# PE transposes for short segments, a doubling step in pairs, and a factor moved, in a planned fp32 decoder kernel

## The chip, the cores and the metric

One core of one Trainium2 chip runs the kernel. The metric is the device time of one execution in microseconds (us), the median of several executions. Engines are named as the profile names them: PE (TensorE matmul) with PEld (its weight loads), DVE (VectorE), ACT (ScalarE), POOL (GpSimd) and SP (the queue that issues most transfers).

## The reference

One inference step of a one-layer hybrid decoder, all in fp32. A prompt of 16 meta tokens and 512 tokens and a sample group of 8 sequences of 4 tokens go through the layer together, so the kernel works on 560 columns (544 after the meta tokens are dropped).

```python
h = rms_norm(x, g_mix)
proj = h @ w_in        # GLU a | GLU b | q | k | v | z | beta | decay | gate_conv | gate_delta
c = silu(layer_norm(depthwise_conv31(glu_a * sigmoid(glu_b)) + b_dw)) @ w_cout
q, k, v = split(silu(depthwise_conv4(qkv)))      # 8 heads x 128, q and k L2-normalised
# gated delta rule in chunks of tokens; per head, with state S (128 x 128):
M = beta * (k @ k.T) * decay;  A = tril(M, -1) + I
value, kcum = solve(A, [v * beta, k * beta * exp(G)])
u = value - kcum @ S
o = (q * exp(G)) @ S + ((q @ k.T) * decay) @ u
S = S * exp(G_last) + (k * exp(G_last - G)).T @ u
x = x + (sigmoid(gate_c) * c + sigmoid(gate_d) * (rms_norm(o) * silu(z)) @ w_dout) @ w_o
x = x + relu(rms_norm(x) @ w_up) ** 2 @ w_down
```

The prompt's rows start from S = 0; the 8 sample sequences start from states that are read in, 8 x 8 x 128 x 128 numbers, and are written back updated.

## The kernel before, in words

**Large products.** Every weight matrix is cut into chunks of 128 output channels. A chunk's fp32 weights are split into a rounded high part (`wh`) and the remainder (`wl`), the activations likewise, and three products are added: in `gemm` (L613) 88 chunks of 8 x 3 x 2 matmuls of 272 to 280 columns, each one pass; in `up_gemm` (L2083) and `dn_gemm` (L2234) the channel mixer in the same manner. `weights_prep` makes `wl` of a chunk in one of two ways: for chunks `A0` to `A1` - 1 ACT writes -`wh` and POOL issues a transfer that adds the weights to it (L579, L581); for the others DVE subtracts (L585). Results go to two PSUM tiles `pg` in turn, which an evacuation empties.

**The delta rule** uses fp32 matmuls on small tiles; one such matmul stands in the trace as two records. The prompt is solved in segments of 128 tokens (4 per head, the index j), the 48 leftover columns (32 sample, 16 meta) as a fifth. `solve` inverts 32x32 blocks on DVE, `doubling` joins them to 64 and then 128: in its second step 32 matmuls of 64x64 read rows 0 to 63 and write partitions 64 to 127 (L1108), their results are copied out by ACT and DVE in turn, and 32 more read rows 64 to 127 and write partitions 0 to 63 (L1119). `head_prep` turns k and v of a head into token rows: the full segments by PE transposes (L1452, L1461), the short ones (`v4`, `k4`) by matmuls against the identity (L1411, L1413). It also makes `at` = (k.q) * s * D from the products of L1469 (L1473, four DVE operations) and `kd`, k scaled by s * ed. `chain` walks the four segments of a head: k S and q S (L1503, L1505), R = v - ... (DVE, L1509), T R (L1518), u copied out by ACT (L1520), kd u (L1522) and at u (L1525), the new S and the output o (DVE L1529, L1532; for j = 0 DVE L1535 and ACT L1537). The four 128-column quarters of one PSUM bank `bx` hold these results; L1503 writes the quarter that L1525 wrote in the step before, so it also waits until o was read from it. Then come the sample sequences: their states `S0` (read by a transfer, L1599) enter matmuls (L1546), and `decode_state` scales them (ACT L1626), adds the update (PE L1621, DVE L1629) and stores them (L1634); the next head's states are read into the same place after that store has landed. `head_post` normalises the head's output and transposes it back (L1660; the short segment by a 48-column matmul, L1669).

**The order of the work.** All of this is written as generators (streams) that a planner, `Weaver`, interleaves when the program is built. Each `op(engine, cost, deps)` has a cost in us; the planner keeps a clock per engine and always takes the stream whose next operation can start first, ties going to the smaller priority. The large products have priority 5 on PE, so small matmuls go between them as soon as the plan says that they can start. What comes out is one fixed sequence per engine; on the chip each engine follows its sequence and waits on semaphores where the plan was wrong. The conv over 31 taps (`conv`, L1217, 240 operations) fills DVE in the same manner.

## Time and profile before

| | us |
|---|---|
| median of 3 runs | 1069.06 (1068.16 to 1070.02) |
| the profiled execution | 1068.65 |
| its span, first to last instruction | 1066.9 |
| PE busy in the span | 1048.2 |
| DVE / ACT busy | 769.4 / 622.9 |

The span is shorter than the time of the same execution by 1.75 us, which lie around it. PE is busy almost always, and the granted clock is 0.995 over the span. Busy time of PE hides how its matmuls overlap (each is busy for some 290 ns and the next starts some 130 ns later), so the distance between the starts of successive rows is what a piece of work takes of PE.

### The profile page before, as it was taken

What the parts mean: (1) busy time and instruction counts of PE and PEld (TensorE: products, weight loads), DVE (VectorE), ACT (ScalarE), POOL (GpSimd) and SP (SyncE); (2) the same over time, 40 slices, a digit from 0 to 9 for tenths busy, and PEclk for the clock granted to TensorE, in tenths of its full rate; (3) what the DMA queues carried; (4) which work ended last, traced back from release to release, by engine and by line L of the source; (5) the groups of instructions that cost most, each with busy time, mean ns of one, the idle gap of its engine ahead of it and who ended that gap; (6) DMA issues with size and microseconds to landing.
All of it is one profiled execution on the core that took longest, in us unless ns stands there. A gap on an engine that the chain in (4) does not pass through costs nothing.

```text
span 1066.9 us, 21819 instructions
## 1 busy us (share of the span) xinstructions
PE 1048.2 (98%) x8835; PEld 1026.1 (96%) x8835; DVE 769.4 (72%) x1360; ACT 622.9 (58%) x1285; POOL 148.1 (14%) x173
## 2 busy tenths in 40 slices
PE   8999999999999999999999999999999999999997
PEld 6988999999999999899999999999999999999996
DVE  5888879788889887788953355778657547746754
ACT  5677334668787878776358424578327426723741
POOL 2067311102211221122111000000000000000000
PEclk9999999999999999999999999999999999999998
DMA  6232687467576566667877522654365365346222
GB/s 213 82 89 70 124 178 164 87 148 161 139 172 164 143 137 156 164 166 182 187 163 158 179 84 91 163 153 117 109 177 129 100 153 149 94 124 164 80 61 84
DMA packets 57872, 145.55 MB, mean 136 GB/s; under 512 B 14612, under 2 KB 20140, under 8 KB 57772
## 3 DMA queue, kind: packets, MB, share of 16 engines
q1 hardware_dynamic: 46828, 104.32, 30.4%
q0 software_dynamic: 10944, 39.85, 23.2%
q8 instruction: 69, 1.13, 0.4%
q14 instruction: 31, 0.25, 0.1%
HBM read 135.14 MB, written 9.01 MB: 135 GB/s over the span
## 4 chain that ended last, share of the span: by engine, by line
PE 87%; DVE 5%; ACT 3%; DMA 3%; issue 2%; SPq 0%; POOL 0%; POOLq 0%; DVEq 0%; ACTq 0%
PE pg L613 42%; PE pg L2234 17%; PE bk L2083 15%; DVE acc L815 1%; DMA pre<-in_sq_dram 1%; DVE V L1217 1%; PE pg L2083 1%; PE bk L1419 1%; PE bk L1518 1%; PE bk L978 1%; DVE of L815 1%; PE bk L1522 1%; PE bk L1503 1%; DMA M<-in_xT_dram 1%; PE bk L1525 1%
## 5 line engine op out<-in xcount | busy, mean ns | idle before, releaser
L613 PE MATMUL pg<-R,wh 128*128 128x280 f32 (+2 forms) x1920 | 279.3, 295 | 1.0 <-ACT pre L803 1.0
L613 PEld LDWEIGHTS pg<-R,wh 128*128 128x128 f32 x1920 | 253.7, 189 | 3.9 <-issue 1.5
L1217 DVE SCALAR_TENSOR_TENSOR V<-V,vec,V 128x512 f32<-128x512 f32 x240 | 180.5, 781 | 2.2
L568 ACT ACTIVATE wh<-wraw 128x1024 fp32r<-128x1024 f32 (+1 forms) x89 | 93.4, 1049 | 94.3 <-PE pg L613 79.3
L613 PE MATMUL pg<-R,wl 128*128 128x280 f32 (+2 forms) x960 | 144.0, 294 | 0.3 <-issue 0.3
L613 PEld LDWEIGHTS pg<-R,wl 128*128 128x128 f32 x960 | 128.5, 189 | 1.8 <-issue 1.4
L581 POOL DMA_DIRECT2D wl<-in_w_dram x60 | 52.6, 876 | 343.8 <-ACT wl L579 252.5
L2014 ACT ACTIVATE whm<-RT 128x512 fp32r<-128x512 f32 x73 | 45.2, 625 | 53.0 <-PE pg L2234 34.8
L579 ACT ACTIVATE wl<-wh 128x1024 fp32r<-128x1024 f32 x60 | 63.5, 1058 | 14.8 <-PE pg L613 12.9
L1969 POOL DMA_DIRECT2D RT<-in_wu_dram x16 | 13.8, 865 | 381.6 <-DMA RT<-in_wu_dram 185.6
L2017 DVE TENSOR_TENSOR wlm<-RT,whm 128x512 fp32r<-128x512 f32 x73 | 49.8, 687 | 16.9 <-issue 8.4
L2234 PE MATMUL pg<-RD,whm 128*128 128x272 f32 (+2 forms) x272 | 57.7, 288 | 0.0
L2234 PE MATMUL pg<-K,whm 128*128 128x272 f32 (+2 forms) x272 | 57.6, 288 | 0.0
L2083 PE MATMUL bk<-R,whm 128*128 128x272 f32 x318 | 54.5, 288 | 0.0
L613 PE MATMUL pg<-K,wh 128*128 128x272 f32 x256 | 53.0, 289 | 0.2 <-DVE K L1766 0.2
L613 PE MATMUL pg<-RD,wh 128*128 128x272 f32 x256 | 53.2, 289 | 0.0
L2234 PE MATMUL pg<-RD,M 128*128 128x272 f32 x264 | 46.2, 288 | 0.0
L2014 ACT ACTIVATE whm<-wrawm 128x512 fp32r<-128x512 f32 x43 | 26.7, 623 | 32.6 <-PE pg L2234 29.7
L2083 PEld LDWEIGHTS bk<-R,whm 128*128 128x128 f32 x318 | 45.6, 189 | 0.0
L585 DVE TENSOR_TENSOR wl<-wraw,wh 128x1024 fp32r<-128x1024 f32 x28 | 35.1, 1253 | 13.5 <-ACT wh L568 9.5
L2234 PE MATMUL pg<-RD,wlm 128*128 128x272 f32 (+2 forms) x272 | 43.5, 289 | 0.0
L2234 PEld LDWEIGHTS pg<-K,whm 128*128 128x128 f32 x272 | 43.5, 188 | 0.0
(524 smaller groups left out, 2442.5 us busy)
## 6 DMA issues: line engine op xcount, KB each, us to landing
wraw<-in_w_dram SPq DMA_DIRECT2D x87, 512.0 KB, 3.8
wl<-in_w_dram POOLq DMA_DIRECT2D x60, 512.0 KB, 5.6
RT<-in_wu_dram SPq DMA_DIRECT2D x24, 512.0 KB, 5.2
RT<-in_wu_dram POOLq DMA_DIRECT2D x16, 512.0 KB, 7.3
wrawm<-in_wn_dram SPq DMA_DIRECT2D x16, 512.0 KB, 3.6
RT<-in_wn_dram SPq DMA_DIRECT2D x16, 512.0 KB, 3.5
M<-in_sd_dram SPq DMA_DIRECT2D x16, 256.0 KB, 3.4
out_osd_dram<-M SPq DMA_DIRECT2D x16, 256.0 KB, 3.8
```

Source lines behind the costliest of these rows:

```text
L568: nc.scalar.activation(wh[:, c[0]:c[1]], w[:, c[0]:c[1]], AF.Copy)
L579: nc.scalar.activation(wl, wh.bitcast(F32), AF.Copy, scale=-1.0)
L581: nc.gpsimd.dma_start(wl, i["w"][n].bitcast(F32R), accum_op=ALU.add)
L585: nc.vector.tensor_tensor(wl, w, wh.bitcast(F32), op=ALU.subtract)
L613: nc.tensor.matmul(pt[:, hf, 0:N], w[idx][:, k, :], x[:, off + hf * N:off + hf * N + N], start=k == 0 and not part and x is hi, stop=k == ...
L815: nc.vector.scalar_tensor_tensor(acc[:, 0:584], pr[:, q:q + 584], vcol(w + q), acc[:, 0:584], op0=ALU.mult, op1=ALU.add)
L1217: nc.vector.scalar_tensor_tensor(cc[:, 0:512], G[r][:, 16 + q:528 + q], vcol(w + q), cc[:, 0:512], op0=ALU.mult, op1=ALU.add)
L1969: nc.gpsimd.dma_start(rb, i["wu"][g][:, 1024:2048], accum_op=ALU.add)
L2014: nc.scalar.activation(hi, raw, AF.Copy)
L2017: nc.vector.tensor_tensor(lo, raw, hi.bitcast(F32), op=ALU.subtract)
L2083: nc.tensor.matmul(acc[an], w[:, kp, :], x, start=kp == 0 and not part and x is hi and m not in (3, 6, 7), stop=kp == 3 and part == 1, ski ...
L2234: nc.tensor.matmul(out, w[:, k % 4, :], x[:, a], start=n_ == 0 and x is hi, stop=n_ == len(STEPS) - 1)
```

## The change

(1) `transpose` in place of a matmul against the identity for `v4`, for `k4` (heads 0 to 6, where it has 96 columns), and for the short segment of the output in `head_post`. (2) In the second doubling step the 32 matmuls of each kind go quarter by quarter, and those of quarters 2 and 3 of the first kind alternate with those of quarters 0 and 1 of the second. (3) The factor s is taken out of `at` and `kd` and put into the copy of u (a scale of the ACT operation that is there anyway); `at` becomes one DVE operation of 512 columns. (4) In `chain` the two quarters `ba` and `bu` change places from step to step, and the wait for the reading of o moves from L1503 to L1518's product. (5) `decode_state` gets priority -2 in place of 1. (6) The planner adds 0.09 us to a large product that follows a small matmul, and takes PE operations by start and priority alone. (7) `A1` is 64 in place of 72: `wl` of the eight `gate_conv` chunks is made by DVE. (8) `mlp_norm` waits for an earlier step.

```diff
@@ Weaver.run
+                if eng == "pe":
+                    key, switch = (start, s[0], s[1]), False
+                    if best is None or key < best[0]:
+                        best = (key, s, eng, start, cost + (0.09 if self.small and tab == "main" else 0.0), tab)
+                    continue
...
-            if tab is not None:
+            if eng == "pe":
+                self.small = tab != "main"
+            elif tab is not None:
                 self.tab = tab
...
-        A0, A1 = 12, 72
+        A0, A1 = 12, 64
...
@@ gemm (up_gemm and dn_product likewise)
-                            t = yield op("pe", 2 * N * 0.4605e-3, tp, tk, tf)
+                            t = yield op("pe", 2 * N * 0.4605e-3, tp, tk, tf, tab="main")
...
@@ kfin
-            t = yield op("dve", 0.2, t)
-            nc.vector.tensor_tensor(st["sk"][:], st["s"][:], st["ed"][:], op=ALU.mult)
...
@@ doubling
-            for m in range(32):
-                t = yield op("pe", 0.058, tn[m // 16], tb)
+            def first(m, cost):
+                tb_[m // 8] = yield op("pe", cost, tn[m // 16], tb)
                 nc.tensor.matmul(B[m // 8][64:128, m % 8, :], KT[0:64, m, 64:128], Tn[0:64, m, :], start=True, stop=True)
...
+            def second(m, cost):
+                q = m // 8
+                tb_[q] = yield op("pe", cost, t1[q], *tc_[2 * (m // 16):2 * (m // 16) + 2])
+                nc.tensor.matmul(B[q][0:64, m % 8, :], P2[m // 16][64:128, m % 16, :], CTT[64:128, m, 64:128],
                                  start=True, stop=True)
...
+            for q in (0, 1):
+                for m in range(8 * q, 8 * q + 8):
+                    yield from first(m, 0.116)
+                yield from keep(q)
+            for q in (2, 3):
+                for m in range(8 * q, 8 * q + 8):
+                    yield from first(m, 0.07)
+                    yield from second(m - 16, 0.07)
+                yield from keep(q)
+                yield from done(q - 2)
+            for q in (2, 3):
+                for m in range(8 * q, 8 * q + 8):
+                    yield from second(m, 0.116)
+                yield from done(q)
...
@@ head_prep
-            yield op("pe", 0.22, tv, tb4)
-            nc.tensor.matmul(b4[:96, 0:128], M2["v4"], ident, start=True, stop=True)
-            yield op("pe", 0.22, tv, tb4)
-            nc.tensor.matmul(b4[:wk, 128:256], k4, ident, start=True, stop=True)
+            yield op("pe", 0.12, tv, tb4)
+            nc.tensor.transpose(b4[:96, 0:128], M2["v4"], ident)
+            yield op("pe", 0.12 if wk > 64 else 0.22, tv, tb4)
+            if wk > 64:
+                nc.tensor.transpose(b4[:wk, 128:256], k4, ident)
+            else:
+                nc.tensor.matmul(b4[:wk, 128:256], k4, ident, start=True, stop=True)
...
-                nc.scalar.activation(kd[:, j, :], b[:, 128 * j:128 * j + 128], AF.Copy, scale=st["sk"][:, hh, j:j + 1])
+                nc.scalar.activation(kd[:, j, :], b[:, 128 * j:128 * j + 128], AF.Copy, scale=st["ed"][:, hh, j:j + 1])
...
-            for j in range(4):
-                t1 = yield op("dve", 0.263, t)
-                nc.vector.scalar_tensor_tensor(at[:, j, :], b[:, 128 * j:128 * j + 128], st["s"][:, hh, j:j + 1],
-                                               Ds[hh][:, j, :], op0=ALU.mult, op1=ALU.mult)
-                E(("at", hh, j)).set(t1)
-                if j == 0:
-                    E(("ready", hh)).set(max(t1, tx))
-                    W.spawn(chain(hh), -1)
+            t1 = yield op("dve", dve_c(512), t)
+            nc.vector.tensor_tensor(at, b.rearrange("p (t c) -> p t c", c=128), Ds[hh], op=ALU.mult)
...
@@ chain
+                ba, bu = (bx[:, 256:384], bx[:, 0:128]) if j % 2 else (bx[:, 0:128], bx[:, 256:384])
                 if j:
-                    t = yield op("pe", 0.22, ts, to)
-                    nc.tensor.matmul(bx[:, 0:128], ks, S, start=True, stop=True)
+                    t = yield op("pe", 0.22, ts)
+                    nc.tensor.matmul(ba, ks, S, start=True, stop=True)
...
-                t = yield op("pe", 0.3, t, t2, tr, tbx)
-                nc.tensor.matmul(bx[:, 256:384], CT["T"][:, 4 * hh + j, :], rr, start=True, stop=True)
+                t = yield op("pe", 0.3, t, t2, to, tr, tbx)
+                nc.tensor.matmul(bu, CT["T"][:, 4 * hh + j, :], rr, start=True, stop=True)
                 tu = yield op("act", 0.17, t)
-                nc.scalar.activation(u, bx[:, 256:384], AF.Copy)
+                nc.scalar.activation(u, bu, AF.Copy, scale=st["s"][:, hh, j:j + 1])
...
-            W.spawn(decode_state(hh, tu), 1)
+            W.spawn(decode_state(hh, tu), -2)
...
@@ head_post
-            t4 = yield op("pe", 0.06, t1, tb4)
-            nc.tensor.matmul(b4[:, 0:48], ob[:, 4, :], ident[:, 0:48], start=True, stop=True)
+            t4 = yield op("pe", 0.12, t1, tb4)
+            nc.tensor.transpose(b4[:, 0:128], ob[:, 4, :], ident)
...
@@ mlp_norm
-            yield wait(("upm", 4, 4))
+            yield wait(("upm", 3, 2))
```

On PE, at the second doubling step, the program had before (`pg` is the PSUM tile of the large products, `bk` a bank of small results, `R`, `wh` and `wl` the large products' operands; a row with x16 is sixteen instructions):

```order
L613 MATMUL pg_2349<-R_29_97,wh_2082 128x280 x4
L1108 MATMUL bk_155_2339<-M_751 64x64 x8
L1108 MATMUL bk_156_2340<-M_751 64x64 x8
L1108 MATMUL bk_157_2341<-M_751 64x64 x8
L1108 MATMUL bk_158_2342<-M_751 64x64 x8
L613 MATMUL pg_2349<-R_29_97,wh_2082 128x280 x12
L1119 MATMUL bk_155_2339<-RT_750,M_751 64x64 x8
L1119 MATMUL bk_156_2340<-RT_750,M_751 64x64 x8
L1119 MATMUL bk_157_2341<-RT_750,M_751 64x64 x8
L1119 MATMUL bk_158_2342<-RT_750,M_751 64x64 x8
L613 MATMUL pg_2349<-R_29_97,wh_2082 128x280 x16
```

And it has now (L1119 is the first kind, L1124 the second, L622 the large products):

```order
L622 MATMUL pg_2236<-R_29_97,wh_2077 128x280 x18
L1119 MATMUL bk_157_2367<-M_790 64x64 x8
L622 MATMUL pg_2236<-R_29_97,wh_2077 128x280 x2
L1119 MATMUL bk_158_2368<-M_790 64x64 x8
L622 MATMUL pg_2236<-R_29_97,wh_2077 128x280 x2
L1119 MATMUL bk_159_2369<-M_790 64x64
L1124 MATMUL bk_157_2367<-RT_789,M_790 64x64
L1119 MATMUL bk_159_2369<-M_790 64x64
L1124 MATMUL bk_157_2367<-RT_789,M_790 64x64
L1119 MATMUL bk_159_2369<-M_790 64x64
L1124 MATMUL bk_157_2367<-RT_789,M_790 64x64
```

The two groups of 32 have become six (two of 8, two of 8 pairs, two of 8), each with large products before and behind it.

On PE, the first steps of head 0's chain were before (`M` holds the head's work tiles, `K` its keys, `RT` the solved T):

```order
L1522 MATMUL bk_177_2675<-M_2462 128x128
L1525 MATMUL bk_177_2675<-M_2462 128x128
L613 MATMUL pg_2713<-R_29_97,wh_2582 128x272 x20
L1503 MATMUL bk_177_2675<-M_2462,K_56_327 128x128
L1505 MATMUL bk_177_2675<-M_2462 128x128
L613 MATMUL pg_2713<-R_29_97,wh_2582 128x272 x8
L1518 MATMUL bk_177_2675<-M_2462,RT_750 128x128
```

They are now (L1546 and L1549 are kd u and at u, L1527 and L1529 are k S and q S, L1542 is T R; between them stand the short segment's instructions of the next head's `head_prep`):

```order
L1546 MATMUL bk_179_2771<-M_2517 128x128
L1549 MATMUL bk_179_2771<-M_2517 128x128
L1434 MATMUL bk_182_2816<-cst_68,M_2517 96x128
L1437 MATMUL bk_182_2816<-cst_68,kq_26_93 96x128
L1441 MATMUL bk_182_2816<-kq_26_93 96x48
L1445 MATMUL bk_182_2816<-ones_71,M_2517 128x1 x4
L1445 MATMUL bk_182_2816<-ones_71,M_2517 96x1
L1527 MATMUL bk_179_2771<-M_2517,K_58_342 128x128
L1529 MATMUL bk_179_2771<-M_2517 128x128
L622 MATMUL pg_2781<-R_29_97,wh_2648 128x274 x8
L1542 MATMUL bk_179_2771<-M_2517,RT_789 128x128
```

Twenty large products stood between at u and the next k S; now eight small matmuls stand there and no large product.

## Rows read from the trace of the kernel before

**Rows 1.** The page, part 1, the line of PE (busy us, share of the span, instructions); and the view by stretches (from:to in us, length, then busy us and instructions of PE, PEld, DVE, ACT, POOL, the granted TensorE clock, the DMA share, GB/s): the preparation of the decay tables and keys, the stretch of the eight heads, the layer norm with the gates and the products behind it.

```profile
PE 1048.2 (98%) x8835; PEld 1026.1 (96%) x8835; DVE 769.4 (72%) x1360; ACT 622.9 (58%) x1285; POOL 148.1 (14%) x173
...
30.00:125.00 95.00, 92.58 (x749) 88.79 (x748) 79.93 (x135) 59.90 (x119) 42.99 (x31) 1.00 0.33 86
200.00:490.00 290.00, 286.19 (x2413) 277.22 (x2413) 242.80 (x478) 226.71 (x612) 58.61 (x70) 1.00 0.65 153
490.00:690.00 200.00, 199.76 (x1588) 198.86 (x1587) 125.03 (x182) 103.32 (x143) 16.64 (x19) 1.00 0.59 149
```

**Rows 2.** The view of waits, engine PE (who waited <- for whom: us in total, times, longest).

```profile
PE bk L1503 <- ACT M L1537: 2.1, 2, 1.5
...
PE bk L1546 <- DMA M<-in_sd_dram: 1.1, 1, 1.1
...
PE pg L613 <- ACT pre L803: 1.0, 1, 1.0
```

**Rows 3.** Timeline of PE at two places of the heads (start us, us until the last end, engine, line, operation, tiles, partitions x columns, form, count of records): matmuls against the identity, and PE transposes.

```profile
206.00 0.38 PE L1411 MATMUL bk<-cst,M 128*96 128x128 f32 x2
206.22 0.38 PE L1413 MATMUL bk<-cst,kq 128*96 128x128 f32 x2
...
272.07 0.49 PE L1461 MATMUL bk<-cst,K 128*128 128x128 f32 x3
272.42 0.49 PE L1522 MATMUL bk<-M 128*128 128x128 f32 x2
```

**Rows 4.** Timeline of PE, around the 48-column matmul of head_post, columns as in the group before.

```profile
264.64 0.32 PE L1669 MATMUL bk<-cst,M 128*128 128x48 f32 x2
264.78 0.76 PE L613 MATMUL pg<-R,wh 128*128 128x280 f32 x4
265.38 0.38 PE L1522 MATMUL bk<-M 128*128 128x128 f32 x2
```

**Rows 5.** The chain that ended last in order of time (start us, us, what, count): the longest piece of nothing but 280-column products.

```profile
115.56 62.97 PE pg L613 x488
```

**Rows 6.** Timeline of PE, the second doubling step.

```profile
190.23 3.94 PE L1108 MATMUL bk<-M 64*64 64x64 f32 x64
194.10 1.82 PE L613 MATMUL pg<-R,wh 128*128 128x280 f32 x12
195.85 3.94 PE L1119 MATMUL bk<-RT,M 64*64 64x64 f32 x64
199.72 0.65 PE L613 MATMUL pg<-R,wh 128*128 128x280 f32 x3
```

**Rows 7.** Timeline of PE, the first doubling step: one record of each of two 32x32 tiles in turn.

```profile
178.96 0.19 PE L1075 MATMUL bk<-M 32*32 32x32 f32 x1
178.99 0.19 PE L1075 MATMUL bk<-M 32*32 32x32 f32 x1
179.02 0.19 PE L1077 MATMUL bk<-M 32*32 32x32 f32 x1
```

**Rows 8.** Groups of instructions by line (line, engine, operation, tiles, form, count | busy us, mean ns of one | idle us before them and what ended it), DVE.

```profile
L1473 DVE SCALAR_TENSOR_TENSOR M<-bk,st_s,RD 128x128 f32<-128x128 f32 x32 | 9.5, 344 | 2.0 <-PE bk L1469 2.0
L1629 DVE TENSOR_TENSOR M<-bk,M 128x512 f32<-128x512 f32 x16 | 11.0, 685 | 2.7 <-ACT M L1626 2.7
L1532 DVE TENSOR_TENSOR M<-bk,M 128x128 f32<-128x128 f32 x24 | 6.8, 282 | 0.0
L585 DVE TENSOR_TENSOR wl<-wraw,wh 128x1024 fp32r<-128x1024 f32 x28 | 35.1, 1253 | 13.5 <-ACT wh L568 9.5 <-ACT sg L434 2.3 <-PE pg L613 1.7
```

**Rows 9.** Timeline of PE and then of ACT in head 0, where a wait is in square brackets (us idle before the row <- what ended it).

```profile
220.64 0.39 PE L1525 MATMUL bk<-M 128*128 128x128 f32 x2
220.78 2.75 PE L613 MATMUL pg<-R,wh 128*128 128x272 f32 x20
225.06 0.49 PE L1503 MATMUL bk<-M,K 128*128 128x128 f32 x2 [1.53 <-ACT M L1537]
...
223.03 0.20 ACT L803 ACTIVATE pre<-pg 128x32 f32<-128x32 f32 x1 [2.24 <-DMA pre<-in_sq_dram]
...
224.75 0.27 ACT L1537 ACTIVATE M<-bk 128x128 f32<-128x128 f32 x1
```

**Rows 10.** Timeline of PE, SP (its rows are issues of transfers) and PE again: the second half of head 5's decode states, from their matmul to the read by head 6.

```profile
435.52 0.51 PE L1621 MATMUL bk<-um,KT 96*128 96x512 f32 x1 [0.17 <-POOL um L1616]
...
440.02 0.42 SPq L1634 DMA_DIRECT2D out_osd_dram<-M  x1
443.83 0.33 SPq L1599 DMA_DIRECT2D M<-in_sd_dram  x1
444.26 0.41 SPq L551 DMA_DIRECT2D wraw<-in_w_dram  x1
...
449.11 0.43 PE L1546 MATMUL bk<-M,kq 128*32 128x128 f32 x8 [1.13 <-DMA M<-in_sd_dram]
```

**Rows 11.** Timeline of PE and then of DVE at one step of the chain in head 3.

```profile
339.21 0.49 PE L1522 MATMUL bk<-M 128*128 128x128 f32 x2
339.54 0.39 PE L1525 MATMUL bk<-M 128*128 128x128 f32 x2
...
341.74 0.38 PE L1503 MATMUL bk<-M,K 128*128 128x128 f32 x2
...
340.03 0.35 DVE L1529 SCALAR_TENSOR_TENSOR M<-M,st_eGl,bk 128x128 f32<-128x128 f32 x1
```

50 lines of the change are left out of this document (22 added, 28 removed).

## The prediction

> **What bounds the kernel now.** I read the page's line of busy times and the view by stretches first: PE is busy 1048.2 of 1066.9 us, at granted clock 1.00 in the stretches shown, and the other engines are well below it [rows 1]. So the time is the sum of what PE has to do, plus the places where PE stands. What PE has to do is read from the distance between starts: in a long piece of nothing but large products a 280-column product takes 62.97 / 488 = 0.129 us [rows 5]. What PE stands is the length of a stretch less its busy time: 2.4 us from 30 to 125, 3.8 us from 200 to 490, where the heads run, and 0.2 us from 490 to 690 [rows 1]. The view of waits then names those places: 2.1 us where L1503 waits for ACT's copy of o (L1537), 1.1 us where the decode states are still being loaded, 1.0 us for an evacuation on ACT in the early stretch [rows 2]. The reader is to see that there are only about 6 us of waits in the region that the change touches; the rest that it can win must be PE work that goes away.
>
> **The change part by part.** I count PE time first.
>
> *Transposes.* An fp32 matmul against the identity starts at 206.00 and the next small one at 206.22: 0.22 us, in two records. Three PE transposes of the same width start at 272.07 and what follows at 272.42: 0.117 us each, one record each [rows 3]. The 48-column matmul of `head_post` is no cheaper: from its start to that of the next small matmul are 0.74 us with four large products in between (0.516), which leaves 0.22 [rows 4]. Its replacement has 128 columns, but one record. So each replacement saves 0.103 to 0.107 us. There are 8 for `v4`, 7 for `k4` and 8 for the output: 23 x 0.105 = 2.4 us, and as PE is the bound nothing hides them.
>
> The Trainium skill (TensorE: Matmul & The Clock Gate, § Terms, under xbus) gives trn2's transpose mode as four times faster for fp32. By that each replacement would save 0.165 us and the 23 would save 3.8 us. This case's rows show a factor of two, 0.117 against 0.22, and the sum goes by the rows.
>
> *Doubling.* 64 records of the first kind take 190.23 to 194.10, 3.87 us, or 0.0605 each; the 12 large products behind them take 1.75 us in place of 12 x 0.129 = 1.55, so 0.20 us go into changing over [rows 6]. A group costs 4.07 us and the two 8.14. Now there are six groups. Four of 16 records cost 4 x (0.97 + 0.20) = 4.7. The two of eight pairs have 16 records of each kind, which use other rows and other partitions. The trace has no such pair of 64x64; the nearest rows are pairs of 32x32, where a record of each of two tiles together take 0.03 us although each is busy for 0.19 [rows 7]. If the 64x64 pair runs side by side it takes 0.0605 us and the step 7.0 us (1.1 less than now); if one behind the other, 0.121 us and 9.0 us (0.8 more). The part of a change-over that may be hidden inside the 3.87 us is paid four times more, at most some 0.16 each, which moves the upper end to 1.5 more. I take side by side, since [rows 7] are the nearer, with half of that hidden part and a little for imperfect overlap: -0.3 us.
>
> *Factor s.* Four DVE operations of 0.344 us become one of about 0.685 (the nearest 512-column one that reads PSUM), 8 times: 11.0 us of DVE become 5.5 [rows 8]. The scale on the copy of u is in an ACT operation that exists. This is worth nothing by itself, because DVE is busy 243 of 290 us there [rows 1] and PE fills with large products meanwhile. It has a price: the chain may only begin after all four segments of `at`, 0.34 us later per head, under the same cover; if a head had no large products to fill with, it would be 8 x 0.34 = 2.7 us.
>
> *Quarters in turn.* L1503 no longer waits for the reading of o; the T R product of that step does, one step later. In head 0, ACT was held until 223.03 by a late transfer, and copied o at 224.75; PE stood 1.53 us until 225.06 [rows 9]. With the change k S could go as soon as DVE has S, and the T R behind it needs o only after a further step of about a microsecond. The 2.1 us of L1503 should go; but a late ACT also holds the other steps (the copy of u is ACT's too), so I keep half: -1.0 us, with bounds -2.1 (all gone) and +1.0 (the same lateness caught at a second step).
>
> *Decode states.* Eight scalings on ACT, two additions on DVE, two matmuls, two POOL operations and two stores on SP per head come earlier in their queues, and with them the next head's two loads. The way from a matmul (435.52) to its store takes 4.5 us, the store 3.8 (440.02 to 443.83), and the load some 5.3 until PE reads at 449.11, 1.13 us late [rows 10]. With the additions right behind the matmul (0.51 + 0.69 us) it is 10.3 us. But in the new order the reader has also come nearer: for head 6 the first four matmuls on the states stand 42 large products and some 3.9 us of small matmuls behind the update, 9.3 us by the same prices. So 1.0 us of wait is replaced by about 1.0 us: 0, with bounds -1.1 and +2.5 (if another two heads, at 10.5 us, miss by 0.7 each). On SP a weights load (444.26) stands behind the load of states [rows 10]; no wait of PE for weights is in the trace, so this order has room.
>
> *A1.* Eight `wl` go to DVE, 8 x 1.25 = 10.0 us [rows 8], in the stretch where DVE is busy 125 of 200 us and PE stands 0.2 [rows 1]: nothing. Without that cover, if each chunk waited for its `wl`, it would be up to 10 us; the later chunks are made this way already and PE does not stand.
>
> *The planner* now reckons 0.09 us for each change from small to large. The trace has no such gap for full-size small matmuls (the 0.74 us are used up) [rows 4], and 0.20 us for the tiled ones [rows 6]. I enter 0 for the changed order as a whole.
>
> The sum: -2.4 - 0.3 - 1.0 = -3.7 us. The profiled execution took 1068.65 us (span 1066.9 and 1.75 around it), which gives 1064.95; it lies 0.4 us under the median of the runs, 1069.06, so for the median I predict **1065.4 us**, with 1063.5 to 1066.8 as the range of this case.
>
> **The rivals.**
>
> *Waits come back.* The order is new almost everywhere, and each wait there [rows 2] is a place where the plan and the chip disagreed by a microsecond. If the new order has as many such places, and the two microseconds of L1503 return as others, only the work that went away remains and part of it is lost again: 2.7 - 1.7 = 1.0 us, **1068.1 us**. For it speaks that late transfers, not the plan, held ACT in head 0 [rows 9], and that stays.
>
> *Everything fits.* If nearly all the 6.2 us that PE stands [rows 1] vanish and the records go too: -8.9 us, **1060.2 us**. Against it: half of those waits lie before the heads, in parts that the change does not treat.
>
> *Slower: the surcharge makes PE early.* A plan with 0.09 us too much for each of some 180 changes puts the chain's matmuls up to 16 us too late on paper, so on the chip PE comes to them early, and each such wait is dead time since PE's order is fixed. A head has about 14 such steps, 112 in all. The change becomes slower by 0.2% if they lose 5.8 us together, 0.052 us each; at 0.07 each it ends at **1073 us**. For it: between at u and the next k S the order now has as little as 0.95 us of work by the rows' prices, where it had at least 1.24. Against it: 339.54 to 340.38 is what that step needs [rows 11], for at u, its end and the DVE operation, less the 0.22 of at u itself, 0.62 us; and the shorter distance is just the DVE reading of o, 0.28 us [rows 8], that k S need no longer wait for.
>
> *The pairs do not overlap.* Then the doubling adds 0.8 to 1.5 us in place of -0.3, and the forecast becomes 1066.5 to 1067.2. I give this 1 in 6 inside the cases.
>
> **How the numbers follow.** Measured against the spread of the three runs, a change of 0.2% (2.1 us) is about what can be told from none: faster means below 1066.9, slower above 1071.2. The forecast has 0.55; everything fits, 0.10; waits come back and its neighbours between 1066.9 and 1071.2, 0.22; slower, 0.13. Faster is 0.65. The range of 1061.0 to 1070.0 leaves out the slower case, the far end of the waits and half of the best case, 2 in 10; it holds the bounds of the unknown terms (-3.0 and +6.3 around the sum together), but for the last 1.7 us above, which need all of them to go wrong at once.
>
> **What would show it.** PE should have 23 fewer records, 8812, and L1434, L1437 (but for head 7) and L1693 one record each, some 0.11 us apart. Alternating L1119 and L1124 should start two records within 0.07 us. The wait of k S (L1527) for ACT should be gone from the view of waits. PE's idle time between 200 and 490 should fall from 3.8 to about 3. The prediction is wrong if the records go and PE's idle time in the heads rises by more than 2 us: then the order, not the work, decides; or if large products of the `gate_conv` chunks wait for DVE's `wl`.

## The result and the profile after

The changed kernel takes **1083.94 us** (median of 4 runs, 1079.79 to 1084.28), the kernel before 1069.45 us beside it: the ratio is 1.0126, interval 1.0103 to 1.0149. It is slower by 14.5 us. The forecast was 1065.4 us, and the time lies outside its range.

The profiled execution took 1083.81 us, its span 1082.0. Page of the changed kernel, part 1 (columns as in [rows 1]):

```profile
span 1082.0 us, 21735 instructions
...
PE 1052.6 (97%) x8812; PEld 1027.7 (95%) x8812; DVE 772.5 (71%) x1343; ACT 620.5 (57%) x1278; POOL 141.3 (13%) x165
```

The 23 records are gone, and PE is nevertheless busy 4.4 us longer than in [rows 1]. The same execution by stretches:

```profile
30.00:125.00 95.00, 89.50 (x702) 85.30 (x701) 75.87 (x121) 56.76 (x114) 41.62 (x29) 0.96 0.30 81
125.00:200.00 75.00, 73.26 (x842) 72.73 (x841) 62.72 (x130) 32.12 (x41) 10.21 (x16) 0.98 0.75 159
200.00:490.00 290.00, 283.67 (x2434) 272.12 (x2434) 242.38 (x464) 226.45 (x608) 58.31 (x67) 0.99 0.62 146
490.00:690.00 200.00, 199.75 (x1589) 198.87 (x1588) 123.31 (x172) 95.50 (x130) 9.86 (x11) 1.00 0.48 130
```

PE stands 5.5 us from 30 to 125 (2.4 before) and 6.3 from 200 to 490 (3.8 before), and the granted clock is no longer 1.00 there [rows 1]. Two things are lost at the same places, then: waits, and clock. The view of waits of PE names the first (line numbers are those of the changed file, about 9 to 25 higher):

```profile
PE bk L1542 <- ACT M L1536: 3.2, 2, 3.0
PE bk L719 <- POOL zs L715: 3.2, 1, 3.2
PE pg L2107 <- DVE V L2166: 2.4, 1, 2.4
PE bk L1099 <- issue: 1.7, 1, 1.7
PE pg L2258 <- DVE V L2274: 1.7, 1, 1.7
PE pg L622 <- DVE R L473: 1.6, 2, 0.9
...
PE bk L1570 <- DMA M<-in_sd_dram: 1.0, 2, 0.7
```

The last has its like in [rows 2], and the first, a wait of the chain for ACT, has one there of 2.1 us in two parts; the other five are new. The second loss is seen in four short stretches, PE alone (length, busy, granted clock, DMA share, GB/s), here first of the changed kernel and then, for the first three, of the kernel before:

```profile
52.00:60.00 8.00, 5.84 (x24) 0.57 0.02 4
196.00:200.00 4.00, 3.70 (x30) 0.57 0.54 101
300.00:306.00 6.00, 3.68 (x19) 0.72 0.67 149
728.00:732.00 4.00, 4.00 (x22) 0.57 0.92 244
...
52.00:60.00 8.00, 8.00 (x64) 1.00 0.31 80
196.00:200.00 4.00, 4.00 (x66) 1.00 0.26 51
300.00:306.00 6.00, 6.00 (x66) 1.00 0.95 226
```

Where the clock is at its lower level (1.2 in place of 2.4 GHz) a stretch loses the missing share of its length: 8 x 0.43 = 3.4, 4 x 0.43 = 1.7, 6 x 0.28 = 1.7 and 1.7 us, 8.5 in all. That is an upper bound, since PE stands for a part of the first three and loses nothing to the clock while it stands. The kernel before is at 1.00 in all four places, and what it loses itself early on, 1.7 us from 10 to 16 us, is not lost in the changed kernel's execution.

To place the 15.1 us between the two spans I count the 7104 large products over PE's records and take the time at which the same one starts in each kernel. The columns are the time to the 768th (the preparation), from there to the 3072nd (doubling, heads, layer norm's start), from there to the 5088th (gates, mixer, first part of the MLP), and the rest of the span.

| kernel | to 768 | heads, to 3072 | to 5088 | rest |
|---|---|---|---|---|
| before | 141.0 | 402.6 | 257.6 | 265.7 |
| changed | 145.7 | 408.7 | 262.5 | 265.1 |
| e1: (6) undone | 138.9 | 398.9 | 261.7 | 265.2 |
| e2: (6) alone | 146.5 | 407.9 | 265.4 | 265.5 |
| e5: addition from the 768th on | 140.1 | 408.5 | 258.2 | 265.5 |
| e6: addition up to the 768th | 146.7 | 403.9 | 263.8 | 265.1 |
| e9: (1) to (5) and (8) | 139.1 | 395.5 | 259.4 | 265.5 |
| e10: (5) alone | 138.9 | 397.4 | 259.9 | 265.1 |
| e15: (1) to (5), -0.04 | 139.8 | 393.9 | 260.3 | 265.1 |

So the changed kernel loses 4.7 us in the preparation, 6.1 in the heads and 4.9 in the middle, though the heads have less to do. The middle is no loss of edit (6): without it, in experiment 1, it takes 261.7 us too. How each place came about can be followed in its trace.

**In the preparation.** Timeline of PE, and then of POOL, columns as in [rows 9]:

```profile
48.30 0.78 PE L622 MATMUL pg<-R,wh 128*128 128x280 f32 x4 [0.86 <-DVE R L473]
49.80 0.53 PE L622 MATMUL pg<-R,wh 128*128 128x280 f32 x2 [0.72 <-DVE R L473]
53.52 0.69 PE L719 MATMUL bk<-zs,crr 128*128 128x384 f32 x1 [3.19 <-POOL zs L715]
...
56.58 3.52 PE L622 MATMUL pg<-R,wl 128*128 128x280 f32 x16
59.94 2.34 PE L622 MATMUL pg<-R,wh 128*128 128x280 f32 x17
```

```profile
45.47 2.09 POOL L748 TENSOR_TENSOR V<-cst,st_gh 128x512 fp32r<-128x512 f32 x1
...
50.61 1.54 POOL L748 TENSOR_TENSOR V<-cst,st_gl 128x512 fp32r<-128x512 f32 x1
52.10 1.36 POOL L715 TENSOR_TENSOR zs<-cst,st_gh 128x384 fp32r<-128x384 f32 x1
```

The first PE row of `g_stage` stands behind 326 large products in the order of before, and behind 166 now. PE therefore comes to the decay tables while POOL still makes them: L719 waits 3.2 us for `zs`, which POOL starts at 52.10 because six products for `V` stand ahead of it. Before, four of them stood ahead of it: POOL's own order has moved with PE's, and no run holds one of the two fixed. Sixteen large products then take 3.36 us (56.58 to the next row at 59.94), 0.21 each in place of the 0.129 of [rows 5].

**In the heads.** ACT ahead of the 3.0 us wait of PE at 302.32:

```profile
296.20 1.06 ACT L588 ACTIVATE wl<-wh 128x1024 fp32r<-128x1024 f32 x1
300.60 0.20 ACT L812 ACTIVATE pre<-pg 128x32 f32<-128x32 f32 x1 [3.34 <-DMA pre<-in_sq_dram]
...
301.91 0.35 ACT L1536 ACTIVATE M<-bk,st_eG 128x128 f32<-128x128 f32 x1
```

This is [rows 9] again: a transfer holds ACT at an evacuation, and the chain's small copy (L1536) stands behind it. The other long wait in this column of the table, 1.7 us at L1099, lies in the first doubling step: it ends at 196.30, in the midst of 32x32 matmuls, and the profile names nothing that ended it. All five kernels that have the addition in the preparation (the changed one, experiments 2, 6, 12 and 14) wait there for 1.7 to 2.7 us, and no other does; the cause stays open.

**In the middle.** DVE ahead of the wait at 725:

```profile
719.54 0.72 DVE L2214 TENSOR_TENSOR K<-acc,RD 128x544 fp32r<-128x544 f32 x1
725.02 0.69 DVE L2021 TENSOR_TENSOR RT<-RT 128x512 f32<-128x512 f32 x1 [4.76 <-DMA RT<-in_wu_dram]
...
726.87 0.43 DVE L2166 TENSOR_TENSOR V<-Ex,pg 128x272 f32<-128x272 f32 x1
```

An addition that needs a late transfer stands ahead of the evacuation (L2166) for which PE waits. This wait is not the change's own: experiments 1 and 8 have it at 2.7 and 3.2 us with the old rule, and experiment 7 has it at 3.2 us in the very order of before.

### The profile page after: what moved, and what is told of

Its sections match the earlier page's. It is cut to its first block, busy times and chain, and to the rows that moved or that the text cites. A ratio compares the mean times of both kernels' runs of the same rounds, so it can differ in the third digit from the quotient of the medians.

```text
span 1082.0 us, 21735 instructions
## 1 busy us (share of the span) xinstructions
PE 1052.6 (97%) x8812; PEld 1027.7 (95%) x8812; DVE 772.5 (71%) x1343; ACT 620.5 (57%) x1278; POOL 141.3 (13%) x165
## 4 chain that ended last, share of the span: by engine, by line
PE 85%; issue 4%; DMA 3%; ACT 3%; DVE 3%; POOL 2%; SPq 0%; POOLq 0%; DVEq 0%; ACTq 0%
PE pg L622 43%; PE pg L2258 17%; PE bk L2107 14%; DMA M<-in_sd_dram 1%; POOL V L748 1%; DMA RT<-in_wu_dram 1%; PE bk L987 1%; PE bk L1494 1%; PE bk L1546 1%; POOL um L1640 1%; PE bk L1542 1%; PE pg L2107 1%; PE bk L1549 0%; DMA M<-in_xT_dram 0%; PE bk L1527 0%
## 5 line engine op out<-in xcount | busy, mean ns | idle before, releaser
L622 PE MATMUL pg<-R,wh 128*128 128x280 f32 (+2 forms) x1920 | 282.3, 296 | 1.7 <-DVE R L473 1.6
L622 PEld LDWEIGHTS pg<-R,wh 128*128 128x128 f32 x1920 | 256.5, 190 | 5.4 <-DVE R L473 2.0
L1240 DVE SCALAR_TENSOR_TENSOR V<-V,vec,V 128x512 f32<-128x512 f32 x240 | 173.2, 749 | 3.4 <-ACT V L1231 1.1
L622 PE MATMUL pg<-R,wl 128*128 128x280 f32 (+2 forms) x960 | 144.0, 296 | 0.0
L622 PEld LDWEIGHTS pg<-R,wl 128*128 128x128 f32 x960 | 129.2, 191 | 0.8 <-issue 0.6
L590 POOL DMA_DIRECT2D wl<-in_w_dram x52 | 45.6, 877 | 339.7 <-ACT wl L588 240.3
L594 DVE TENSOR_TENSOR wl<-wraw,wh 128x1024 fp32r<-128x1024 f32 x36 | 44.7, 1243 | 37.1 <-PE pg L622 16.7
L588 ACT ACTIVATE wl<-wh 128x1024 fp32r<-128x1024 f32 x52 | 55.0, 1058 | 12.5 <-PE pg L622 10.2
L622 PE MATMUL pg<-K,wh 128*128 128x272 f32 x256 | 53.2, 289 | 0.2 <-DVE K L1790 0.2
L622 PE MATMUL pg<-RD,wh 128*128 128x272 f32 x256 | 53.0, 288 | 0.0
L2258 PEld LDWEIGHTS pg<-RD,whm 128*128 128x128 f32 x272 | 43.4, 188 | 1.9 <-issue 1.9
```

The source lines that it names most:

```text
L588: nc.scalar.activation(wl, wh.bitcast(F32), AF.Copy, scale=-1.0)
L590: nc.gpsimd.dma_start(wl, i["w"][n].bitcast(F32R), accum_op=ALU.add)
L594: nc.vector.tensor_tensor(wl, w, wh.bitcast(F32), op=ALU.subtract)
L622: nc.tensor.matmul(pt[:, hf, 0:N], w[idx][:, k, :], x[:, off + hf * N:off + hf * N + N], start=k == 0 and not part and x is hi, stop=k == ...
L1240: nc.vector.scalar_tensor_tensor(cc[:, 0:512], G[r][:, 16 + q:528 + q], vcol(w + q), cc[:, 0:512], op0=ALU.mult, op1=ALU.add)
L2258: nc.tensor.matmul(out, w[:, k % 4, :], x[:, a], start=n_ == 0 and x is hi, stop=n_ == len(STEPS) - 1)
```

## The experiments

Theory A after the two traces: edit (6) lays PE's rows so that PE comes too early to the work of the others, and each long wait is followed by a stretch at the lower clock. The first rival (B): the edits in the heads make the waits. Edit (8) needed no run: with it undone the changed kernel's program is the same row for row, and so are that of before with (8) alone and that of experiment 9 without it. So the kernels that have it may be compared with those that don't (experiments 4, 10 and 13 to 15).

**Experiment 1, edit (6) undone.**

```diff
-                if eng == "pe":
-                    key, switch = (start, s[0], s[1]), False
...
-                            t = yield op("pe", 2 * N * 0.4605e-3, tp, tk, tf, tab="main")
+                            t = yield op("pe", 2 * N * 0.4605e-3, tp, tk, tf)
```

> The changed kernel with edit (6) alone undone: the planner chooses PE's operations as it did before (patience and rank count again, no 0.09 us for a large product behind a small one). All other edits stay. Theory A (the order decides): the new choice laid the early stage and the heads so that PE waits for late work of the other engines (in the changed kernel 3.2 us for zs at 53.5 us, 1.6 us for R at 47 to 49, 3.0 us for M at 302), and each long wait is followed by a stretch at a lower granted clock; with the old choice most of that goes and what the edits save on TensorE stays: 1065 to 1071 us, no PE wait over 2 us before 500 us. Rival B (the edits in the heads themselves, the one `at` operation, the alternating quarters and the decode states' priority, make the waits): 1078 to 1084 us, with the 3.0 us wait in the heads still there.

1065.68 us (1063.92 to 1066.49), ratio to before 0.9954 (0.9939 to 0.9969). One edit makes 18 us, and without it the change is a gain. By stretches:

```profile
30.00:125.00 95.00, 93.30 (x755) 89.66 (x755) 81.69 (x136) 59.23 (x119) 44.26 (x31) 1.00 0.35 87
...
200.00:490.00 290.00, 285.66 (x2408) 277.05 (x2407) 234.77 (x454) 231.82 (x616) 59.27 (x61) 1.00 0.67 156
```

The clock is back at 1.00 in both, and no wait over 2 us is left ahead of 500 us.

**Experiment 2, edit (6) alone on the kernel before.** The same lines, added.

> The kernel before with edit (6) alone: the same work, record for record, in the order that the new choice gives. Theory A (the order decides): slower than before by 5 to 15 us, 1074 to 1084 us, with new PE waits of over 2 us. Rival B (the heads' edits make the waits): within 2 us of the kernel before, 1067 to 1071 us.

1088.07 us (1084.32 to 1090.57), ratio 1.0164 (1.0134 to 1.0194): worse than the upper end, with the same work as before. The waits of the preparation are the same to a tenth (PE, 30 to 125 us):

```profile
PE bk L719 <- POOL zs L715: 3.2, 1, 3.2
PE pg L622 <- DVE R L473: 1.6, 2, 0.9
```

Rival B falls. Experiment 2 has a wait besides that the changed kernel hasn't: 2.5 us for `wl` of a `gate_conv` chunk, one of the eight that edit (7) gives to DVE.

```profile
PE pg L622 <- DMA wl<-in_w_dram: 2.5, 1, 2.5
```

**Experiment 3, edit (1) alone, in the order of before.**

```diff
-            nc.tensor.matmul(b4[:96, 0:128], M2["v4"], ident, start=True, stop=True)
+            nc.tensor.transpose(b4[:96, 0:128], M2["v4"], ident)
...
-            nc.tensor.matmul(b4[:, 0:48], ob[:, 4, :], ident[:, 0:48], start=True, stop=True)
+            nc.tensor.transpose(b4[:, 0:128], ob[:, 4, :], ident)
```

> The kernel before with edit (1) alone, and with the costs that the planner is told left at the old values, so that every engine runs the same operations in the same order; only 23 products against the identity take one record in place of two. Theory A: the whole saving of the records reaches the end, 23 x 0.105 = 2.4 us: 1066.3 to 1067.3 us where the kernel before stands at 1069.1. Rival C (PE is not what sets the end in the heads; what it saves turns into waiting): 1068.5 to 1069.5 us, with PE's idle time between 200 and 490 us about 2 us longer than the 3.8 us of before.

1069.67 us (10 runs, 1066.04 to 1075.92), ratio 1.0004 (0.9983 to 1.0024): no gain that can be told. In the profiled execution, the fastest of the ten, the heads take 401.4 us (402.6 before), so half of the 2.4 us arrives there; PE stands 4.4 us from 200 to 490, 0.6 more than before, where rival C said 2 more. The wait for the states' load tells where some of the rest is, 2.0 us where [rows 2] have 1.1:

```profile
PE bk L1549 <- DMA M<-in_sd_dram: 2.0, 2, 1.5
```

PE is earlier, the transfer isn't. That is rival C in part.

**Experiment 4, edits (1) to (4).** Experiment 1 with, in addition,

```diff
-        A0, A1 = 12, 64
+        A0, A1 = 12, 72
...
-            W.spawn(decode_state(hh, tu), -2)
+            W.spawn(decode_state(hh, tu), 1)
...
-            yield wait(("upm", 3, 2))
+            yield wait(("upm", 4, 4))
```

> The kernel before with edits (1) to (4), and with none of (5) to (8): transposes, pairs in the doubling, s in the copy of u, quarters in turn; planner's rule, A1, decode states' priority and the norm's wait as before. The order still differs from that of before, since the planner is told the new costs. Theory A (the rule and with it the order cost the time): 1063 to 1068 us. Rival B (the heads' edits make the waits): 1075 us or more. Rival D (any new order of this kernel loses some us, since the old one had been found by trying): 1069 to 1076 us, with PE waits of 1 to 3 us at new places in it.

1070.40 us (10 runs, 1067.26 to 1074.72), ratio 1.0009 (0.9992 to 1.0025): neither A nor B, but the lower end of D. The heads take 402.5 us; their waits for `in_sd` come to 2.9 us, the longest 2.2 us.

**Experiments 5 and 6, the addition late or early only.**

```diff
-                        best = (key, s, eng, start, cost + (0.09 if self.small and tab == "main" else 0.0), tab)
+                        best = (key, s, eng, start, cost + (self.extra if self.small and tab == "main" else 0.0), tab)
...
+                if idx == 16:
+                    W.extra = 0.09
```

(`extra` starts at 0; in experiment 6 it starts at 0.09 and becomes 0.)

> The changed kernel, with the 0.09 us that the planner adds to a large product behind a small one counted only from the 17th chunk on (after 768 large products, ahead of the doubling and the heads); before that the addition is 0, which gives the early stage the order that it has with the old choice (g_stage's first PE row behind 326 large products, where the changed kernel has it behind 166). Theory A (two separate losses, about 5 us in the early stage and 5 us in the heads, each from PE waiting for work that the planner now lays too close behind): the early waits for zs (3.2 us) and R (1.6 us) are gone, the heads lose some us: 1068 to 1075 us. Rival E (the heads wait only because the early stage ran differently): 1064 to 1067 us, as with the old choice throughout.

> The other half: the 0.09 us count up to the 17th chunk only, and are 0 in the doubling and the heads. Theory A (two separate losses): the early waits for zs and R are there as in the changed kernel, with a stretch at a lower granted clock behind them, and the heads lose nothing more: 1069 to 1074 us. Rival E (all of the loss starts in the early stage): 1078 to 1085 us.

1075.30 us (1074.10 to 1079.31), ratio 1.006 (1.0036 to 1.0084), and 1079.97 us (1077.62 to 1081.26), ratio 1.0093 (1.0066 to 1.0119). The first lies just above theory A's range. The table shows the two losses apart: with the late addition the preparation is near that of experiment 1 (1.2 us more) and the heads take 9.6 us more; with the early one the preparation takes 7.8 us more and the heads 5.0. The early one is dearer than theory A said: some 3.6 of the 5.0 us are the unexplained wait in the first doubling step, 2.0 us here, and the stretch at the lower clock behind it (197.4 to 200.8 us); rival E named its time (1078 to 1085 us), but falls on the first of the two. In experiment 5 the heads have no wait over 1.5 us and no slow stretch, the clock is 1.00 from 200 to 490; the loss is in many small delays, of which the view of waits (200 to 490 us) shows the largest:

```profile
PE bk L1549 <- ACT M L1547: 2.4, 4, 1.5
PE bk L1530 <- ACT M L1564: 1.7, 3, 1.2
```

Counted over PE's records in the heads, starts that come 0.3 to 1 us behind the one before (large products follow each other by 0.126, small ones by less) are 14 before, 11 in experiment 1, 29 in experiment 5 and 28 in the changed kernel; they take 5.7, 3.7, 12.8 and 12.2 us.

**Experiment 7, four waits put into the kernel before.**

```diff
+            for k, n in STALL.get((q, c), ()):
+                a = fhl[8 * q + k][0]
+                nc.scalar.activation(a[:, 0:n], a[:, 0:n].bitcast(F32), AF.Copy)
             for n_, (part, k) in enumerate(STEPS):
```

> The kernel before, with four waits put into the down projection, where PE otherwise does nothing but large products at the full clock: ahead of a product's first matmul ScalarE copies an operand onto itself that the product before read last, and then one that this product reads first (16 columns each ahead of the first, 544 columns twice ahead of the second, four times ahead of the third, six times ahead of the fourth). The planner isn't told, so that the order is that of before. By the 0.6 us of such a copy and some 0.4 us of handing over, PE should wait about 0.8, 1.7, 3.0 and 4.3 us, 9.8 us in all. Theory A (a wait of 2 us and more is paid twice: itself, and a stretch behind it in which the granted clock is at the lower level and large products start every 0.23 us in place of 0.126): 1082 to 1092 us, the clock below 1 behind the third and fourth, and at 1 behind the first. Rival F (the clock falls for a cause other than the waits): 1077 to 1080 us, products every 0.126 us behind all four.

1081.42 us (2 runs, 1084.25 and 1078.59), ratio 1.0114 (1.007 to 1.0157). The first wait came out at 0.29 us; the others, in the timeline of PE and by stretches behind each:

```profile
871.56 1.27 PE L2240 MATMUL pg<-M,whm 128*128 128x272 f32 x8 [1.35 <-ACT M L2230]
...
946.58 0.52 PE L2240 MATMUL pg<-RD,M 128*128 128x272 f32 x2 [2.67 <-ACT RD L2230]
...
970.47 0.52 PE L2240 MATMUL pg<-RD,M 128*128 128x272 f32 x2 [4.04 <-ACT RD L2230]
```

```profile
869.00:874.00 5.00, 3.65 (x29) 1.00 0.55 161
947.00:951.00 4.00, 4.00 (x22) 0.57 0.37 131
970.00:975.00 5.00, 4.54 (x24) 0.66 0.92 207
```

Behind 1.35 us the clock stays; behind 2.67 and 4.04 us it falls, and 1.7 us are lost each time (4 x 0.43, 5 x 0.34), no more behind the longer one. Theory A's second half holds: 8.4 us of waits and 3.4 of clock make 11.8, and from the 5088th large product to the end the profiled execution takes 277.6 us, 11.9 more than before. (The two runs lie 8.8 and 14.4 us above before, so their median says less; the profiled one, the longer, has the middle's wait of 3.2 us and another 1.7 us of clock besides.) The length of a wait alone doesn't decide: experiment 1's wait of 2.67 us in the middle and experiment 4's of 2.2 us in the heads have the clock at 1.00 behind them, while it falls behind the changed kernel's 1.7 us in the first doubling step.

**Experiment 8, edit (5) undone in experiment 1.**

```diff
-            W.spawn(decode_state(hh, tu), -2)
+            W.spawn(decode_state(hh, tu), 1)
```

> The kernel of the first experiment (all edits but the planner's rule) with edit (5) undone too: the decode states' update has priority 1 again in place of -2. The prediction took 0 for edit (5) with bounds -1.1 to +2.5. If that holds: 1063.5 to 1067.5 us. Rival G (the priority is what makes the first experiment faster than the kernel with edits (1) to (4) alone): 1068.5 to 1071.5 us, with waits for in_sd's transfer of 1 to 3 us.

1070.71 us (10 runs, 1066.38 to 1072.05), ratio 1.0004 (0.9987 to 1.0021): rival G, with the wait that it names (200 to 490 us):

```profile
PE bk L1561 <- DMA M<-in_sd_dram: 3.0, 2, 1.8
```

**Experiments 9 and 10, edit (5) with (1) to (4), and alone.** Experiment 9 is experiment 4 with this edit (and with edit (8)), experiment 10 the kernel before with it:

```diff
-            W.spawn(decode_state(hh, tu), 1)
+            W.spawn(decode_state(hh, tu), -2)
```

> The kernel before with edits (1) to (5): the first experiment with edit (7) undone too (A1 is 72 again). Its order is that of the first experiment up to the last heads. Theory A (order and rule cost the time, and edit (5) is what lets the saving of edits (1) to (4) come through): 1063 to 1067 us, heads (from the 768th to the 3072nd large product) in 398 to 400 us as in the first experiment, where the kernel before takes 402.6. Rival H (edit (7) is what the first experiment gained by): 1068 to 1071 us.

> The kernel before with edit (5) alone: the same work, the decode states' update with priority -2 in place of 1, and so another order from the first heads on. Rival G (the priority by itself takes out the waits for in_sd's transfer and what they hold up): 1065 to 1067 us, heads 399 to 400 us. Theory I (there is no single cause: any new order of this kernel moves the heads by some us either way, and the first experiment drew a good one): anywhere from 1066 to 1075 us.

1063.82 us (6 runs, 1060.37 to 1066.18), ratio 0.995 (0.993 to 0.997), and 1065.54 us (10 runs, 1063.04 to 1068.55), ratio 0.9969 (0.9955 to 0.9983). Heads by stretches, first of 9 and then of 10:

```profile
200.00:490.00 290.00, 288.32 (x2434) 280.39 (x2434) 237.75 (x458) 232.97 (x618) 60.20 (x63) 1.00 0.67 158
```

```profile
200.00:490.00 290.00, 287.38 (x2445) 280.99 (x2445) 237.59 (x478) 226.67 (x613) 60.70 (x57) 1.00 0.67 157
```

PE stands 1.7 and 2.6 us there, 3.8 before [rows 1], and no wait for `in_sd` is left in either. The priority alone is worth 3.6 us; between experiments 4 and 9, which differ by it (and by edit (8), which moves nothing), 6.6, and between 8 and 1, 5.0. In the heads of experiment 10 PE stands 1.2 us less than before. PE also leaves the large products less often there, 134 times where it was 151, but that explains no more: a full-size small matmul has no gap of its own [rows 4], and the 0.20 us of [rows 6] are those of the tiled ones, whose number is the same. What makes the rest of the 3.6 us is not shown. Edit (7) can't be told apart by experiments 1 and 9, whose intervals overlap.

**Experiment 11, equal work, another order.** Experiment 1, with the old costs told for the transposes.

```diff
-            yield op("pe", 0.12, tv, tb4)
+            yield op("pe", 0.22, tv, tb4)
...
-            t4 = yield op("pe", 0.12, t1, tb4)
+            t4 = yield op("pe", 0.06, t1, tb4)
```

> The first experiment's work, instruction for instruction; only the costs that the planner is told for the three transposes are the old ones (0.22, 0.22 and 0.06 us in place of 0.12, 0.12 and 0.12), which gives another order from the heads on. Rival G (edit (5) with the saved records makes 1065.7 us): 1064 to 1067 us. Theory I (the order within the heads is worth some us either way, at equal work): more than 1.5 us away from 1065.7, most likely above it: 1067 to 1075 us, with PE's starts 0.3 to 1 us late more often than the 11 times of the first experiment (28 in the changed kernel).

1063.96 us (1063.49 to 1065.74), ratio 0.9958 (0.9942 to 0.9974). That is 1.7 us from experiment 1 and just below the range of rival G, but measured against the kernel before beside each of them the two are the same (0.9958 and 0.9954). Theory I, that any order is a draw worth some us, has no support here; one other order can't rule it out. Starts 0.3 to 1 us late are 20 here, and none is later, so their number alone doesn't give the time.

**Experiment 12, a third of the addition.**

```diff
-                        best = (key, s, eng, start, cost + (0.09 if self.small and tab == "main" else 0.0), tab)
+                        best = (key, s, eng, start, cost + (0.03 if self.small and tab == "main" else 0.0), tab)
```

> The changed kernel with 0.03 us in place of 0.09 us added to a large product behind a small one. In the order g_stage's first PE row stands behind 166 large products again, as with 0.09 (326 without the addition). Theory A (it is a threshold: the early stage's loss comes whole as soon as the order flips, however small the addition): the waits for zs and R between 45 and 58 us are there in full, the early stage (to the 768th large product) ends at 145 to 147 us where the kernel before is at 141.0 and the first experiment at 138.9, and the whole takes 1073 to 1081 us. Rival J (the loss grows with the size of the addition): about a third of it, 1069 to 1073 us.

1083.28 us (1080.80 to 1088.75), ratio 1.0145 (1.0103 to 1.0186), above theory A's range: the loss is there in full. The preparation takes 148.6 us and the heads 406.9. Rival J falls: the loss is no smaller at 0.03 than at 0.09 us. Where between 0 and 0.03 it sets in was not tried.

**Experiments 13 and 14, the two halves of edit (6)**, each on experiment 9. First the choice by start and priority without the addition, then the addition with the old choice:

```diff
+                if eng == "pe":
+                    key, switch = (start, s[0], s[1]), False
...
+                        best = (key, s, eng, start, cost + (0.0 if self.small and tab == "main" else 0.0), tab)
```

```diff
+                if eng == "pe":
+                    rank = start + (self.patience if s[0] == 4 else 0.6 if s[0] == 2.5 else 0.0)
+                    key, switch = (rank, s[0], s[1]), False
...
+                        best = (key, s, eng, start, cost + (0.09 if self.small and tab == "main" else 0.0), tab)
```

> The kernel with edits (1) to (5) (the ninth experiment), and of edit (6) the choice of PE's operations by start and priority alone; nothing is added to a large product. The order is that of the ninth experiment up to the mixer, where the rows of mlp_norm move. Theory A (the addition of 0.09 us makes the loss, the choice by start alone costs no more than the 1.7 us for which PE waits for the first results of the down projection in all four kernels so far that have it, and in none without it): 1064 to 1067 us, with that wait. Rival M (the choice makes a good part of the 18 us): 1070 us or more.

> The same kernel (edits 1 to 5) with the other half of edit (6): 0.09 us are added to a large product behind a small one, and patience and rank count for PE as before. The order is that of the changed kernel up to the last heads, with the last small rows of the heads behind 2934 large products (3080 in the ninth experiment). Theory A: 1079 to 1084 us, the waits for zs and R in the early stage, the late starts in the heads, and no 1.7 us wait at the first results of the down projection. Rival M: below 1075 us.

1065.05 us (10 runs, 1063.09 to 1068.11), ratio 0.9963 (0.9943 to 0.9982), and 1084.34 us (1079.04 to 1088.38), ratio 1.0135 (1.0094 to 1.0176). `g_stage` stands behind 326 large products in the first and behind 166 in the second. The addition makes the loss. That the 1.7 us wait at L2274 belongs to the choice was wrong: experiment 14 has it too.

**Experiment 15, the opposite sign.** On experiment 14:

```diff
-                        best = (key, s, eng, start, cost + (0.09 if self.small and tab == "main" else 0.0), tab)
+                        best = (key, s, eng, start, cost + (-0.04 if self.small and tab == "main" else 0.0), tab)
```

> The kernel with edits (1) to (5), and 0.04 us taken off a large product behind a small one, in place of the 0.09 us added; patience and rank count. The plan then lays more large products between small ones that depend on each other: the last small rows of the heads stand behind 3128 large products, where it is 3080 in the ninth experiment and 2934 in the changed kernel. Theory K (the large products laid between are the reserve that hides what the plan underrates in the other engines' latencies; the addition took it away): as fast as the ninth experiment or faster, 1061 to 1065 us, with no more starts 0.3 to 1 us late in the heads than its 12. Rival L (any shift of PE's price spoils the order, whichever way): 1067 us or more.

1061.97 us (6 runs, 1060.91 to 1064.45), ratio 0.9936 (0.9915 to 0.9956), the fastest of all, though its interval overlaps with that of experiment 9. Heads by stretches:

```profile
200.00:490.00 290.00, 288.99 (x2457) 281.87 (x2457) 237.02 (x454) 232.90 (x618) 60.65 (x71) 1.00 0.67 158
```

PE stands 1.0 us there, 10 starts are 0.3 to 1 us late, and the heads take 393.9 us. Rival L falls. Theory K's forecast came true, but not all of its reason. The place that the expectation gives (3128, 3080, 2934) is the layer norm's first mean, behind the heads; the heads' own last rows stand behind 2622, 2578 and 2600 large products. Counted at the chain itself, of its 115 to 123 groups of PE rows those with at most eight large products ahead of them are 66 in experiments 1 and 9 and 67 here, and 75 in the changed kernel and experiment 14, 79 in experiments 5 and 12. So the addition does take cover from the chain (large products laid ahead of a step that has to wait for another engine), as K says, and of these seven the four with less cover are the slow ones (heads of 406.9 to 412.3 us against 393.9 to 398.9). The same holds for the work of before, where edit (6) raises the count from 57 to 69 (experiment 2). But the count doesn't give the time: experiment 11 has 67 with heads of 398.3 us, experiment 6 has 70 with 403.9, and the kernel before, with 57, takes 402.6. That less cover is how the addition costs time in the heads is therefore argued, not shown; taking 0.04 us off gives no more cover than none, and shows only that a shift of PE's price does no harm in this direction.

## Why the prediction was wrong

- **The step that failed: "I enter 0 for the changed order as a whole".** Edit (6) costs 18 us beside the other edits (1065.68 against 1083.94) and 19 alone. The prediction reasoned about whether the 0.09 us are a true price of a large product. What counts is what the plan does with it: it thinks PE slower, lays at most eight large products ahead of 75 of the chain's groups where it was 66 (experiment 15's count), moves `g_stage` from 326 to 166, and on the chip PE gets there first and waits. That the addition does it is shown (experiments 1, 2, 13 and 14), for the preparation by the named waits too; for the heads the way in which it does is argued.
- **The rival "the surcharge makes PE early" had the mechanism**, at 0.13 and 1073 us. In the heads of experiment 5 it was also near in size: 408.5 - 398.9 = 9.6 us over 112 steps is 0.086 each, in many small delays, where it said 0.07. In the changed kernel the loss is not spread like that: two places, waits of 1.7 and 3.0 us with up to 1.7 us of clock behind each, hold up to 8.1 us. The rival left out the preparation, where one flip of the order (166 for 326) costs 6.8 us against experiment 1, and the clock.
- **The clock was in no term.** By the missing share of the clock 11.2 us are lost over the changed execution and 5.4 over that of before (summed over stretches of 2 us), of which 8.5 and 1.7 lie ahead of the last 25 us.
- **Transposes.** 8812 records as said, and one takes 0.11 us, as the starts of two in turn show. The 2.4 us were right as PE work, but as time no gain can be told from the runs (experiment 3); part of it became a longer wait for `in_sd`.

```profile
269.00 0.27 PE L1434 MATMUL bk<-cst,M 128*96 128x128 f32 x1
269.11 0.27 PE L1437 MATMUL bk<-cst,kq 128*96 128x128 f32 x1
```

- **Doubling.** The pairs run side by side, as taken: two starts within 0.01 us, the next pair 0.06 later.

```profile
203.64 0.22 PE L1119 MATMUL bk<-M 64*64 64x64 f32 x1
203.65 0.22 PE L1124 MATMUL bk<-RT,M 64*64 64x64 f32 x1
203.70 0.22 PE L1119 MATMUL bk<-M 64*64 64x64 f32 x1
```

  Six groups of 1.27 us net make 7.6 in place of 8.1 in the same counting: -0.5 where -0.3 stood.
- **Quarters in turn.** The wait of k S for ACT is gone, and PE waits for ACT at later steps: the bound "the same lateness caught at a second step". In the changed kernel it is T R (L1542, 3.2 us, for the copy of q S at L1536). With the old rule T R waits 0.8 us in experiments 1 and 9, and kd u, the step behind it, waits for the copy of u, 3.2 us in experiment 1 and 0.6 in experiment 9. In experiment 1 (L1533 is T R, L1537 kd u):

```profile
PE bk L1537 <- ACT M L1535: 3.2, 2, 1.7
...
PE bk L1533 <- ACT M L1527: 0.8, 1, 0.8
```

  No run has edit (4) alone, so its price stays open.
- **Decode states first.** Entered as 0 with -1.1 as the best; beside the old rule it is worth 3.6 to 6.6 us. The mis-sized step is "the reader has also come nearer": that holds for the changed kernel's own order, where PE waits 1.0 us for `in_sd` as said, but no reader waits any more in experiments 1, 9 and 10. The waits for `in_sd` (1.1 to 3.0 us in experiments 4, 8 and before) are only a part of that worth; the rest has no row.
- **Factor s and A1** show no wait of their own: none of PE for `wl` or for `at` is among the waits of the changed kernel. Under the new order A1 may even gain: the wait for `wl` in experiment 2 is for one of its chunks.
- **The sum** for all but the planner, 1065.4 us, is what experiment 1 measures (1065.68), but by luck: edits (1) to (4), taken at 3.7 us, gain nothing that can be told (experiment 4, ratio 1.0009), and edit (5), taken at 0, makes the gain. Its own sign of failure was met: PE's idle time in the heads rose by 2.5 us with the records gone.

## What to carry to other kernels

Where an order is fixed ahead of time, a planner's cost is not a neutral estimate: charging the bound engine more took cover from between dependent steps here and flipped the order elsewhere, so price such an edit as a new program, stage by stage, and not as zero. Change work and order apart, since here one told constant undid every saving. Before counting saved records as time, look at what the engine waits for next; here that was a transfer, and giving it priority was worth more than the records.

## What the runs showed of the hardware

- A wait of PE can be paid for twice. Put in by hand between large products, 2.67 and 4.04 us (experiment 7) were each followed by 1.7 us lost at the lower clock, 1.35 us by none. The length doesn't decide alone: in the changed kernel the clock also fell behind 1.7 us amid 32x32 matmuls (196.30) and 2.4 us amid large products (727.71), and stayed at 1.00 behind 2.67 us in experiment 1.
- PE transposes of 128 columns in fp32 cost one record and about 0.11 us, half of the 0.22 us of the matmul against the identity. Two 64x64 matmuls of the two kinds, on other rows and other partitions, started 0.01 us apart and cost no more than one.
- The 512-column products on POOL (L748) took 1.04 us each in the first two rows from 43.47 on and 1.54 to 2.09 us in the next four. DVE was idle beside the first, busy for 0.82 us beside the second with operations that read PSUM, and busy all the time beside the other four, mostly with operations on two SBUF tiles; whether that is why was not tried.
